# Two side-by-side recurrence lanes, one PSUM bank each, in layer 0 of a hybrid RWKV / gated-delta trunk

## The chip, the cores and the metric

The kernel runs on one core of a Trainium2 chip. The metric is the device time of one execution, in microseconds; a measurement is the median of several executions. The engines are called as in the profile: PE is TensorE (matmuls; PEld are its weight loads), DVE is VectorE, ACT is ScalarE, POOL is GpSimd and SP is SyncE, which issues most DMAs.

## The reference

A two-layer streaming encoder over 1024 frames of width 1024. Layer 0 is the one that matters here. One input projection feeds two groups of heads:

```
A = RWKV-7: 8 heads x 64        state = state*w + (state a) b' + v k' ; y = state r   (per frame)
B = gated DeltaNet: 4 heads x128  chunkwise WY form, state carried from chunk to chunk
out = concat(A, B) @ w_out, then MLP and a gated per-layer embedding
```

For group A the reference scans frame by frame (`wkv7_scan`). For group B it works on chunks: it solves a unit lower triangular system in each chunk, then runs

```
v_new = uc - wc @ state
o     = qd @ state + qkc @ v_new
state = state * gl + kd' @ v_new
```

over the chunks in order. The kernel treats both groups in the same way, in chunks of 128 frames: all that a chunk needs besides the incoming state is prepared ahead (scores, an inverse of a triangular matrix, decays), and a short chain of products carries the state through the chunks.

## The kernel before, in words

All matrix products of the projections are done with operands split in a high and a low part (tiles `whi`, `wlo`, `xg`), in 128x512 pieces into PSUM tiles called `dps` ("dense" work). PSUM has eight banks of 2 KB per partition, and here two are for dense work (tag `dense`), two for transposes and sums (tag `tp`), and one each for `ch`, `iz`, `pm` and `y`.

Layer 0 works on 16 units. A unit is a pair of RWKV heads or one gated-delta head (`p` is 0 to 3) in one half of the frames (`hf` is 0 or 1, 512 frames, four chunks); RWKV and gated-delta units alternate (`units`, L539). Each unit goes through five stages, written as Python generators that yield at places where the engine order may switch to something else:

- *in* (`l0_in`): the projections of the unit, the dense work. At the start of each half, x is loaded, scaled and split, and two low-rank projections ("lora", tiles `lwa` and `lg`) are made. Two weights, `wa2` and `g2` (128x512 each), are loaded once, in the first half.
- *front*: decays, normalised keys, score matrices, the first steps of the inverse.
- *mid* (`inverse_end`): the rest of the inverse, written into the tile `F`. There is one `F` for eight blocks (RWKV) and one for four (gated delta), in bank `iz`.
- *back* (`rwkv_back`, `gdn_back`): the chain over the four chunks.
- *post*: normalisation, gate, store to `yd`.

A lane (`l0_lane`) takes the units through one stage, in order. `Trunk.run` sets the order in which instructions are issued on all engines at once: it keeps a clock of its own, in which only matmuls advance time, and goes on with the first lane in its list whose due time has come; a yield says by name how long the lane should stay away, from a table of latencies (`"rwkv_back4": 0.64` and so on). Lanes earlier in the list have priority. Before, the list is post, back, mid, front (two lanes, for even and odd units), the sums for the gated-delta decays, and in. So there is one back lane: the RWKV and gated-delta chains follow one another. Mid may be two units ahead of back (`slack` 2).

The chain of one RWKV chunk (L949 to L990). The scaled state `Sh` is made by DVE (L953) from `S`; the products into `pw` (two with the scores `PMQ`, one with `Sh`) are copied by ACT to `W` (L963); the products of `X` (the inverse) with `W` give `pu`, which DVE scales into `U` (L971); the products of `tm` (transposed keys) with the values and `U` give `pu2`, from which DVE makes the new state (L987). Five more products per chunk give the outputs in `py`. `pw`, `pu` and `pu2` are tiles of bank `ch`, one after the other; `py` is a tile of bank `y` and holds the outputs of all four chunks, until ACT copies it once per unit to a tile `o` (L995) and squares it from PSUM into another (L997). The function `scores` (PMQ, L931) of the next chunk is called between.

The chain of one gated-delta chunk (L1142 to L1160). `pw` is one product of the keys with the state `Sg`; DVE makes `W` (L1147); `pu` is the inverse times `W`; ACT scales it to `U` (L1152); `p2` is the product of the keys with `U`, from which DVE makes the state in place (L1158); two products per chunk go to `po` in bank `y`, copied and squared once per unit (L1163, L1165). `pw`, `pu` and `p2` are tiles of bank `ch` here too, so that the two kinds of chain share both banks.

Every matmul is recorded on the helper's line L177, every transpose on L192; a matmul of two f32 operands appears as two records. The helper `together` ties matmuls in a given order without a semaphore.

Of the kernel before, what the change touches and what calls it, by code (L numbers as in the profile page):

```python
# [8 lines left out]
F32 = mybir.dt.float32  # L9
# [22 lines left out]
L0_BACK = {"gate": 2, "b": 14, "tm": 3, "o": 3}  # L32
# [77 lines left out]
class Trunk:  # L110
    def __init__(self, ctx, tc, a, dbg=None, stop=None):
        self.ctx, self.tc, self.nc, self.a = ctx, tc, tc.nc, a
        self.dbg, self.stop = dbg or {}, stop

        self.now, self.done, self.lat = 0.0, {}, LAT
        self.nd, self.rx, self.late, self.extra = -1, None, None, []

        self.steps, self.begun = [], None
# [385 lines left out]
    def layer0_in(self):  # L504
        nc, tc, a = self.nc, self.tc, self.a
        with ExitStack() as es:
# [60 lines left out]
    def l0_in(self, units):  # L567
# [3 lines left out]
        for u, (nm, p, hf) in enumerate(units):  # L571
            if u % 8 == 0:
# [25 lines left out]
                if hf == 0:  # L598
                    self.wa2 = fr.tile([P, 512], F32, tag="wa2", name="wa2")
                    nc.sync.dma_start(out=self.wa2, in_=a["wa2"])  # L600
                    self.g2 = self.l0.tile([P, 512], F32, tag="g2", name="g2")
                    nc.sync.dma_start(out=self.g2, in_=a["g2"])
# [6 lines left out]
                if hf == 0:  # L609
# [3 lines left out]
                    self.extra = [lambda t=t: self.psm.tile([P, HB], F32, tag=t, name="dps") for t in ("y", "ch", "pm")]  # L613
# [184 lines left out]
    def rwkv_front(self, p, hf, sc, raws, u):  # L798
# [20 lines left out]

        psw, psa = ptile(), ptile()  # L820
        self.together([self.mm(ps, self.wa2[r, p * P:(p + 1) * P], sc["lwa"][r], start=True, stop=True)
# [88 lines left out]
    def rwkv_mid(self, p, hf, sc, st, u):  # L910
        yield from self.inverse_end(st["X"], st["N"], 8, self.F[8])
        return dict(st, F=self.F[8])

    def rwkv_back(self, p, hf, sc, st, u):
# [33 lines left out]
        py = psm.tile([P, HB], F32, tag="y", name="py")  # L948

        for c in range(4):  # L950
# [7 lines left out]
            pw = psm.tile([P, HB], F32, tag="ch", name="ch")  # L958
            for h in range(2):
                self.mm(pw[:, hs[h]], pmq[c, h][:, 1, :], Vt[:, c, hs[h]], start=h == 0, stop=False)  # L960
            self.mm(pw[:, 0:P], AR[:, c, 0, :], Sf, start=False, stop=True)
            W = h2.tile([P, P], F32, tag="W", name="W", bufs=2)
            A.copy(W, pw[:, 0:P])  # L963
# [3 lines left out]
            pu = psm.tile([P, HB], F32, tag="ch", name="ch")  # L967
            U = h2.tile([P, P], F32, tag="U", name="U", bufs=2)
            for h in range(2):
                self.mm(pu[:, hs[h]], X[:, 4 * h + c, :], W[:, hs[h]], start=True, stop=True)  # L970
            V.tensor_tensor(U.rearrange("p (h i) -> p h i", h=2), pu[:, 0:P].rearrange("p (h i) -> p h i", h=2),  # L971
                            cc[:, 2 * c:2 * c + 2].rearrange("p (h o) -> p h o", o=1).broadcast_to((P, 2, 64)),
                            op=ALU.mult)
            py_c = py[:, c * C:(c + 1) * C]
            self.mm(py_c, Sf, AR[:, c, 1, :], start=True, stop=False)
            yield "rwkv_back5"

            pu2 = psm.tile([P, HB], F32, tag="ch", name="ch")
# [7 lines left out]
            S2 = h2.tile([P, 64], F32, tag="S2", name="S2", bufs=2)  # L986
            V.scalar_tensor_tensor(S2, S, ee[:, c:c + 1], pu2[:, 0:64], op0=ALU.mult, op1=ALU.add)  # L987
            S = S2
# [5 lines left out]
        yc = t2(tag="o")  # L994
        A.copy(yc, py)  # L995
        sy = t2(tag="o")
        A.activation(sy, py, AF.Square)  # L997
# [3 lines left out]
    def rwkv_post(self, p, hf, sc, st, u):  # L1001
        nc, sm, V = self.nc, self.sm, self.nc.vector
        t2 = self.t2
        yc, sy, bon = st["yc"], st["sy"], st["bon"]
        pv = self.post_bank()
# [18 lines left out]
        self.mm(pg, self.g2[:, p * P:(p + 1) * P], sc["lg"], start=True, stop=True)  # L1024
# [107 lines left out]
    def gdn_mid(self, n, hf, sc, st, u):  # L1132
        yield from self.inverse_end(st["X"], st["N"], 4, self.F[4])
        return dict(st, F=self.F[4])

    def gdn_back(self, n, hf, sc, st, u):
# [4 lines left out]
        po = psm.tile([P, HB], F32, tag="y", name="po")  # L1141
        for c in range(4):  # L1142
            i = c
            pw = psm.tile([P, HB], F32, tag="ch", name="ch")
            self.mm(pw[:, 0:P], KQ[:, c, 0, :], S, start=True, stop=True)
            W = h2.tile([P, P], F32, tag="W", name="W", bufs=2)
            V.scalar_tensor_tensor(W, pw[:, 0:P], sc["egc"][:, i, n:n + 1], vt[:, c, :], op0=ALU.mult, op1=ALU.add)  # L1147
            yield "gdn_back0"
            pu = psm.tile([P, HB], F32, tag="ch", name="ch")
            self.mm(pu[:, 0:P], X[:, c, :], W, start=True, stop=True)  # L1150
            U = h2.tile([P, P], F32, tag="U", name="U", bufs=2)
# [949 lines left out]
```

## Time and profile before

| | us |
|---|---|
| median of 3 runs | 3112.31 |
| lowest and highest | 3107.09, 3116.35 |
| the profiled execution | 3119.22 |
| its span in the profile | 3117.5 |
| mean granted TensorE clock | 0.968 |

The profile is of one execution. Its span runs from the first to the last instruction, and 1.7 us of the execution lie outside it. The page gives busy times by engine; a view of waits says which instruction an engine stood idle for, and which engine's work ended that wait; a view of windows gives busy times and clock by stage; a view of lines groups equal instructions; the timeline shows single instructions. An interval of idle time in square brackets at the end of a timeline row is the time for which that engine was idle ahead of it.

### The profile page before, as it was taken

What the parts mean: (1) busy time and instruction counts of PE and PEld (TensorE: products, weight loads), DVE (VectorE), ACT (ScalarE), POOL (GpSimd) and SP (SyncE); (2) the same over time, 40 slices, a digit from 0 to 9 for tenths busy, and PEclk for the clock granted to TensorE, in tenths of its full rate; (3) what the DMA queues carried; (4) which work ended last, traced back from release to release, by engine and by line L of the source; (5) the groups of instructions that cost most, each with busy time, mean ns of one, the idle gap of its engine ahead of it and who ended that gap; (6) DMA issues with size and microseconds to landing.
All of it is one profiled execution on the core that took longest, in us unless ns stands there. A gap on an engine that the chain in (4) does not pass through costs nothing.

```text
span 3117.5 us, 47104 instructions
## 1 busy us (share of the span) xinstructions
PE 2998.6 (96%) x17288; PEld 2477.6 (79%) x17288; DVE 2222.7 (71%) x4518; ACT 1512.2 (49%) x2922; POOL 534.0 (17%) x978
## 2 busy tenths in 40 slices
PE   7999999999999999999999999999899999999999
PEld 5777777777777788888887988888788788888887
DVE  6646675667758788877866676776768688888862
ACT  4323433344436544544433577777766545444431
POOL 6524442443510000000005111110210000000002
PEclk8989999999999999999999999999999999999999
DMA  4212112212356444754424111110256444754433
GB/s 137 71 42 72 44 58 72 63 51 70 103 168 206 148 156 150 259 168 153 126 98 136 52 33 33 42 46 16 71 176 215 147 152 149 246 179 147 135 108 102
DMA packets 187639, 358.45 MB, mean 115 GB/s; under 512 B 45712, under 2 KB 47888, under 8 KB 187408
## 3 DMA queue, kind: packets, MB, share of 16 engines
q1 hardware_dynamic: 158608, 303.00, 30.0%
q10 hardware_dynamic: 28800, 52.44, 4.4%
q8 instruction: 136, 2.23, 0.3%
q14 instruction: 95, 0.78, 0.1%
HBM read 262.04 MB, written 93.32 MB: 114 GB/s over the span
## 4 chain that ended last, share of the span: by engine, by line
PE 81%; DVE 9%; ACT 4%; DMA 3%; issue 1%; POOL 1%; SPq 0%; DVEq 0%; POOLq 0%; ACTq 0%
PE dps L177 68%; PE ch L177 2%; PE po L177 2%; PE iz L177 1%; PE pm L177 1%; PE tp L177 1%; PE pt L192 1%; DVE ptile L350 1%; PE py L177 1%; PE sn L177 1%; DVE pb L1941 1%; ACT pb L1954 1%; PE pp L177 1%; DMA wraw<-in_w_out 1%; PE st L177 1%
## 5 line engine op out<-in xcount | busy, mean ns | idle before, releaser
L177 PE MATMUL dps<-r,act 128*128 128x512 f32 x3528 | 831.5, 393 | 0.0
L177 PEld LDWEIGHTS dps<-r,act 128*128 128x128 f32 x3528 | 664.8, 189 | 146.7
L177 PE MATMUL dps<-xg,whi 128*128 128x512 f32 x1280 | 439.7, 424 | 12.7 <-ACT xg L352 7.4
L1598 POOL TENSOR_TENSOR pn<-pn,prs 128x512 f32<-128x512 f32 x32 | 45.0, 1409 | 1577.1 <-ACT prs L386 1480.0
L177 PE MATMUL dps<-wq,act 128*128 128x384 f32 x1536 | 306.4, 345 | 6.9 <-DVE vs L1850 3.1
L177 PEld LDWEIGHTS dps<-xg,whi 128*128 128x128 f32 x1280 | 237.2, 198 | 64.8 <-ACT xg L352 7.4
L177 PEld LDWEIGHTS dps<-wq,act 128*128 128x128 f32 x1536 | 266.7, 191 | 11.1 <-DVE vs L1850 5.3
L177 PE MATMUL dps<-xg,wlo 128*128 128x512 f32 x640 | 260.1, 407 | 1.3 <-DVE wlo L304 1.3
L177 PE MATMUL dps<-late,act 128*128 128x512 f32 x960 | 229.2, 392 | 0.0
L177 PEld LDWEIGHTS dps<-late,act 128*128 128x128 f32 x960 | 180.3, 188 | 39.7
L1271 ACT CAST act<-act 128x512 fp32r<-128x512 f32 (+1 forms) x223 | 137.6, 649 | 129.3 <-PE dps L177 60.7
L1374 DVE TENSOR_TENSOR late<-late,dps 128x512 f32<-128x512 f32 x224 | 152.3, 684 | 62.5 <-PE dps L177 54.2
L1271 ACT CAST act<-late 128x512 fp32r<-128x512 f32 x210 | 124.1, 618 | 136.3 <-PE dps L177 91.1
L177 PE MATMUL dps<-act 128*128 128x512 f32 x672 | 165.5, 393 | 0.1
L1272 DVE TENSOR_TENSOR act<-act 128x512 fp32r<-128x512 f32 (+1 forms) x223 | 154.5, 719 | 4.2 <-ACT act L1271 4.2
L177 PEld LDWEIGHTS dps<-xg,wlo 128*128 128x128 f32 x640 | 125.9, 197 | 32.1 <-issue 2.3
L177 PEld LDWEIGHTS dps<-act 128*128 128x128 f32 x672 | 126.1, 188 | 29.2 <-DVE xw L1506 0.5
L1272 DVE TENSOR_TENSOR act<-late,act 128x512 fp32r<-128x512 f32 x210 | 141.4, 687 | 10.9 <-ACT act L1271 9.0
L303 ACT CAST whi<-wraw 128x1024 fp32r<-128x1024 f32 x78 | 81.9, 1050 | 122.4 <-PE dps L177 83.2
L1506 DVE TENSOR_TENSOR xw<-xw,dps 128x512 f32<-128x512 f32 x174 | 117.7, 681 | 29.6 <-PE dps L177 29.6
L177 PE MATMUL dps<-xw,act 128*128 128x512 f32 x576 | 138.4, 391 | 0.0
L1379 ACT ACTIVATE late<-late 128x512 f32<-128x512 f32 x128 | 80.2, 629 | 117.1 <-DVE late L1374 106.8
(482 smaller groups left out, 5652.0 us busy)
## 6 DMA issues: line engine op xcount, KB each, us to landing
hb<-late ACTq DMA_DIRECT2D x168, 256.0 KB
act<-hb SPq DMA_DIRECT2D x138, 256.0 KB
late<-in_w SPq DMA_DIRECT2D x60, 512.0 KB
wraw<-in_w_in SPq DMA_DIRECT2D x56, 512.0 KB
act<-in_w SPq DMA_DIRECT2D x96, 256.0 KB
braw<-hb SPq DMA_DIRECT2D x72, 256.0 KB
wraw<-in_w_out SPq DMA_DIRECT2D x21, 512.0 KB
wraw<-in_w_qkv SPq DMA_DIRECT2D x21, 512.0 KB
```

Source lines behind the costliest of these rows:

```text
L177: return self.begin(self.nc.tensor.matmul(out, lhsT, rhs, start=start, stop=stop, skip_group_check=again))
L192: return self.begin(self.nc.tensor.transpose(out, in_, ident))
L303: nc.scalar.copy(hi, raw)
L350: nc.vector.tensor_tensor(dst[:, 1, sl], src, dst[:, 0, sl].bitcast(F32), op=ALU.subtract)
L1271: A.copy(hi, s)
L1272: V.tensor_tensor(lo, s, hi.bitcast(F32), op=ALU.subtract)
L1374: V.tensor_tensor(r, t, u, op=ALU.add)
L1379: A.activation(t, t, AF.Relu)
L1506: V.tensor_tensor(x[n][:, hs[hf]], x[n][:, hs[hf]], ps, op=ALU.add)
L1598: G.tensor_tensor(pn, pn, prs[:, sl], op=ALU.mult)
L1941: V.tensor_tensor_reduce(S, pn[:, 0:nn * P], toep[:, (3 - nn) * P:], op0=ALU.add, op1=ALU.max, scale=1.0, scalar=NEG, accum_out=mx[:, 0:1])
L1954: A.activation(S, S, AF.Exp, bias=mx[:, 2:3], accum_out=l[:, 0:1])
```

## The change

1. *Lanes.* The back lane becomes two: one for the even units (RWKV), one for the odd (gated delta). Mid may now be four units ahead of back. The planner's list of lanes whose steps it notes (`ahead`) grows by one.
2. *Banks.* RWKV's chain keeps bank `ch`, gated delta's gets `cg` in place of `y`. Each holds its four products of a chunk in four regions of 128 columns: `pw`, `pu`, `pu2` (or `p2`), and the output (`py`, `yo`). A new helper `behind` ties all matmuls into one of these banks in their order of issue.
3. *Outputs.* ACT copies the output of each chunk (128x128) from the bank to the tile `o`; the square reads that tile.
4. *Order in a chunk.* RWKV: the state `S2` is made ahead of the five output products. Gated delta: the state is made behind both output products.
5. *Tiles.* Two inverse tiles of each size, used in turn (`F[8, e]`, `F[4, e]`, the first of them in the tile of the pool `pre` with the tag `pl`). `W` and `U` have one buffer each, and gated delta its own (`Wg`, `Ug`); `tm` goes from three to two buffers, `o` from three to five.
6. *Loads.* `wa2` and `g2` are loaded for each RWKV unit as 128x128 pieces. Since `pl` is taken, the x tiles of the second half come through `ph` (two of four) and `wraw`, and those for the squares through `ph` alone.

```diff
-L0_BACK = {"gate": 2, "b": 14, "tm": 3, "o": 3}
+L0_BACK = {"gate": 2, "b": 14, "tm": 2, "o": 5}
...
+    def behind(self, key, ins):
+
+        if key in self.last:
+            self.together([self.last[key], ins])
+        self.last[key] = ins
...
-            self.F = {G: l0.tile([P, G, P], F32, tag=f"F{G}", name=f"F{G}") for G in (4, 8)}
+            self.F = {(G, e): l0.tile([P, G, P], F32, tag=f"F{G}{e}", name=f"F{G}") for G, e in ((4, 0), (4, 1), (8, 1))}
+            self.F[8, 0] = self.pre.tile([P, 8, P], F32, tag="pl", name="F8")
...
-            self.run([self.l0_lane(units, "post", "back", 0), self.l0_lane(units, "back", "mid", 0), self.l0_lane(units, "mid", "front", 2),
+            self.run([self.l0_lane(units, "post", "back", 0), self.l0_lane(units, "back", "mid", 0, 0, 2),
+                      self.l0_lane(units, "back", "mid", 0, 1, 2), self.l0_lane(units, "mid", "front", 4),
                       self.l0_lane(units, "front", "in", 0, 0, 2), self.l0_lane(units, "front", "in", 0, 1, 2),
-                      self.gdn_cums(), self.l0_in(units)], ahead=(1, 2))
+                      self.gdn_cums(), self.l0_in(units)], ahead=(1, 2, 3))
...
-                    x2 = [self.load_x(q, self.pre if q < 2 else self.wp, "ph" if q == 0 else "pl" if q == 1 else "wraw")
-                          for q in range(4)]
+                    x2 = [self.load_x(q, self.wp if q in (1, 2) else self.pre, "wraw" if q in (1, 2) else "ph") for q in range(4)]
...
-                    x2 = self.load_x(q, self.pre, "pl" if q % 2 else "ph")
+                    x2 = self.load_x(q, self.pre, "ph")
...
+        wa2 = fr.tile([P, P], F32, tag="wa2", name="wa2")
+        nc.sync.dma_start(out=wa2, in_=self.a["wa2"][:, p * P:(p + 1) * P])
...
@@ rwkv_back, one chunk @@
-        py = psm.tile([P, HB], F32, tag="y", name="py")
+        bank = psm.tile([P, HB], F32, tag="ch", name="ch")
+        pw, pu, pu2, py = bank[:, 0:P], bank[:, P:2 * P], bank[:, 2 * P:2 * P + 64], bank[:, 384:512]
+        yc = t2(tag="o")
...
-            self.mm(py_c, Sf, AR[:, c, 1, :], start=True, stop=False)
             yield "rwkv_back5"
...
                 for h in range(2):
-                    self.mm(pu2[hs[h], 0:64], t[:, c, hs[h]], v[:, hs[h]], start=t is Ktm, stop=t is Btm)
+                    mm(pu2[hs[h]], t[:, c, hs[h]], v[:, hs[h]], start=t is Ktm, stop=t is Btm)
+            S2 = h2.tile([P, 64], F32, tag="S2", name="S2", bufs=2)
+            V.scalar_tensor_tensor(S2, S, ee[:, c:c + 1], pu2, op0=ALU.mult, op1=ALU.add)
+            S = S2
+            mm(py, Sf, AR[:, c, 1, :], start=True, stop=False)
             for v, j in ((Vt[:, c], 2), (U, 0)):
                 for h in range(2):
-                    self.mm(py_c[hs[h]], v[:, hs[h]], pmq[c, h][:, j, :], start=False, stop=j == 0)
+                    mm(py[hs[h]], v[:, hs[h]], pmq[c, h][:, j, :], start=False, stop=j == 0)
+            A.copy(yc[:, c * C:(c + 1) * C], py)
...
-        A.copy(yc, py)
         sy = t2(tag="o")
-        A.activation(sy, py, AF.Square)
+        A.activation(sy, yc, AF.Square)
...
+        g2 = self.l0.tile([P, P], F32, tag="g2", name="g2")
+        nc.sync.dma_start(out=g2, in_=self.a["g2"][:, p * P:(p + 1) * P])
...
@@ gdn_back, one chunk @@
-            yo = po[:, c * C:(c + 1) * C]
-            self.mm(yo, S, qd[:, c, :], start=True, stop=False)
-            p2 = psm.tile([P, HB], F32, tag="ch", name="ch")
-            self.mm(p2[:, 0:P], kd[:, c, :], U, start=True, stop=True)
-            V.scalar_tensor_tensor(S, S, sc["egl"][:, i, n:n + 1], p2[:, 0:P], op0=ALU.mult, op1=ALU.add)
-            self.mm(yo, U, QK[:, c, :], start=False, stop=True)
+            mm(p2, kd[:, c, :], U, start=True, stop=True)
+            mm(yo, S, qd[:, c, :], start=True, stop=False)
+            mm(yo, U, QK[:, c, :], start=False, stop=True)
+            V.scalar_tensor_tensor(S, S, sc["egl"][:, i, n:n + 1], p2, op0=ALU.mult, op1=ALU.add)
+            A.copy(o[:, c * C:(c + 1) * C], yo)
```

More of the change, by code (lines that the diff above doesn't have):

```diff
@@ L598, in l0_in @@
                 if hf == 0:
[L599 to L602, printed above, removed]
                     self.hv = self.l0.tile([P, 2, 4], F32, tag="hv", name="hv")
@@ L611, in l0_in @@
                     self.rs = fr.tile([P, HB], F32, tag="rsbc", name="rsbc", bufs=2)
-                    self.extra = [lambda t=t: self.psm.tile([P, HB], F32, tag=t, name="dps") for t in ("y", "ch", "pm")]
+                    self.extra = [lambda t=t: self.psm.tile([P, HB], F32, tag=t, name="dps") for t in ("cg", "ch", "pm")]
                     self.late, self.plan = [], {2: lambda: self.row_stats([acc], rsc), 3: lambda: self.to_rows(rsc, self.rs)}
@@ L910, in rwkv_mid @@
     def rwkv_mid(self, p, hf, sc, st, u):
-        yield from self.inverse_end(st["X"], st["N"], 8, self.F[8])
-        return dict(st, F=self.F[8])
+        F = self.F[8, u // 2 % 2]
+        yield from self.inverse_end(st["X"], st["N"], 8, F)
+        return dict(st, F=F)
     def rwkv_back(self, p, hf, sc, st, u):
@@ L957, in rwkv_back @@
             Sf = Sh.rearrange("p h i -> p (h i)")
-            pw = psm.tile([P, HB], F32, tag="ch", name="ch")
             for h in range(2):
[L960 to L963, printed above, removed]
+                mm(pw[:, hs[h]], pmq[c, h][:, 1, :], Vt[:, c, hs[h]], start=h == 0, stop=False)
+            mm(pw, AR[:, c, 0, :], Sf, start=False, stop=True)
+            W = h2.tile([P, P], F32, tag="W", name="W")
+            A.copy(W, pw)
             if c < 3:
@@ L1132, in gdn_mid @@
     def gdn_mid(self, n, hf, sc, st, u):
-        yield from self.inverse_end(st["X"], st["N"], 4, self.F[4])
-        return dict(st, F=self.F[4])
+        F = self.F[4, u // 2 % 2]
+        yield from self.inverse_end(st["X"], st["N"], 4, F)
+        return dict(st, F=F)
     def gdn_back(self, n, hf, sc, st, u):
@@ L1140, in gdn_back, with mm @@
         KQ, vt, kd, qd, QK, cs, X = (st[x] for x in ("KQ", "vt", "kd", "qd", "QK", "cs", "F"))
-        po = psm.tile([P, HB], F32, tag="y", name="po")
+        bank = psm.tile([P, HB], F32, tag="cg", name="cg")
+        pw, pu, p2, yo = (bank[:, q * P:(q + 1) * P] for q in range(4))
+        o = self.t2(tag="o")
+        def mm(*args, **kw):
+            self.behind("cg", self.mm(*args, **kw))
         for c in range(4):
             i = c
[L1144 to L1147, printed above, removed]
+            mm(pw, KQ[:, c, 0, :], S, start=True, stop=True)
+            W = h2.tile([P, P], F32, tag="Wg", name="W")
+            V.scalar_tensor_tensor(W, pw, sc["egc"][:, i, n:n + 1], vt[:, c, :], op0=ALU.mult, op1=ALU.add)
```

32 lines of the change are left out of this document (12 added, 20 removed).

## The prediction

> **What bounds the kernel now.** I read the page first, then the waits of TensorE in the first 930 us, then the stages by windows, then the groups by line, and last two short stretches of the timeline. The changed lines belong to layer 0, which fills the span up to about 930 us; everything behind it is untouched.
>
> ```profile
> span 3117.5 us, 47104 instructions
> PE 2998.6 (96%) x17288; PEld 2477.6 (79%) x17288; DVE 2222.7 (71%) x4518; ACT 1512.2 (49%) x2922; POOL 534.0 (17%) x978
> ```
>
> The reader is to see that TensorE (PE) is busy 96% of the whole span: a change of order can win only its idle time, its slow-clock time and the overhead inside its busy time. VectorE (DVE) has room left, ScalarE (ACT) has half its time free.
>
> The windows split the first millisecond. The columns are the length, then for each engine the busy time and the count, then the granted clock, the DMA share and GB/s.
>
> ```profile
> 0.00:30.00 30.00, 20.46 (x75) 15.67 (x76) 15.15 (x18) 16.22 (x25) 25.75 (x86) 0.94 0.56 195
> 30.00:100.00 70.00, 61.05 (x282) 48.19 (x282) 46.91 (x97) 28.76 (x51) 44.07 (x59) 0.90 0.31 92
> 100.00:200.00 100.00, 93.57 (x743) 71.29 (x742) 44.89 (x94) 29.36 (x64) 37.99 (x95) 0.81 0.20 59
> ...
> 300.00:400.00 100.00, 94.62 (x819) 72.57 (x819) 68.10 (x164) 41.90 (x88) 45.64 (x98) 0.92 0.18 54
> ...
> 600.00:700.00 100.00, 98.75 (x924) 74.80 (x924) 61.19 (x148) 40.26 (x89) 43.54 (x114) 0.95 0.18 56
> ...
> 900.00:950.00 50.00, 46.56 (x231) 36.28 (x232) 26.45 (x50) 21.11 (x36) 0.00 (x0) 1.00 0.55 174
> ...
> sum 1000.00, PE 947.69 PEld 735.36 DVE 646.47 ACT 402.77 POOL 384.12; mean PE 78.97 PEld 61.28 DVE 53.87 ACT 33.56 POOL 32.01
> ```
>
> TensorE is idle for 1000 - 947.7 = 52.3 us of the first millisecond, 18.5 us of that before 100 us (30 - 20.46 and 70 - 61.05), where no recurrence runs yet. Some 34 us are left for all of the pipeline's gaps. What ends them is in the waits (time in all, times, longest):
>
> ```profile
> PE dps L192 <- DVE f L714: 8.7, 1, 8.7
> ...
> PE ch L177 <- DVE U L971: 5.6, 7, 2.5
> PE pm L177 <- DVE PMQ L931: 4.1, 5, 1.5
> ...
> PE ch L177 <- DVE Sg L1158: 2.3, 6, 0.9
> ...
> PE ch L177 <- ACT W L963: 1.9, 1, 1.9
> ...
> PE ch L177 <- ACT U L1152: 1.5, 3, 1.1
> ...
> PE pm L177 <- ACT tm L943: 0.7, 1, 0.7
> ...
> PE ch L177 <- DVE S L987: 0.2, 1, 0.2
> ```
>
> All rows but the first belong to the recurrences: 5.6 + 4.1 + 2.3 + 1.9 + 1.5 + 0.7 + 0.2 = 16.3 us in 7 + 5 + 6 + 1 + 3 + 1 + 1 = 24 waits, 0.68 us each. So the chains' latency, which a second lane could cover, costs 16.3 us before, about 0.5% of the span; most of the rest is already hidden behind the projections' matmuls (dps).
>
> **The change part by part.** The price of one link in a chain (last product, reader, next product) has two ends in the trace:
>
> ```profile
> 379.41 0.49 PE L177 MATMUL ch<-Sh,AR 128*128 128x128 f32 x2
> ...
> 379.99 0.27 ACT L963 COPY W<-ch 128x128 f32<-128x128 f32 x1 [1.49 <-PE ch L177]
> ...
> 580.60 0.49 PE L177 MATMUL ch<-Sh,AR 128*128 128x128 f32 x2
> ...
> 582.71 0.62 ACT L893 CAST bh<-f 128x512 fp32r<-128x512 f32 x1 [3.99 <-DVE f L890]
> 583.24 0.26 ACT L963 COPY W<-ch 128x128 f32<-128x128 f32 x1
> ...
> 583.55 0.66 PE L177 MATMUL ch<-W,F 128*128 128x64 f32 x4 [1.86 <-ACT W L963]
> ```
>
> With the reader's engine free, the products end at 379.41 + 0.49 = 379.90 and the copy at 380.26: 0.36 us. With another ScalarE job ahead of it, the products end at 581.09 and the next begin at 583.55: 2.46 us. A link costs what of this no TensorE work between the two products covers.
>
> *Added waits.* Each chain now lives in one bank, and all accesses to it follow each other. In the order of the changed kernel the first product of a next chunk waits for ScalarE's copy of the outputs (27 RWKV and 27 gated-delta places, 24 of each inside a unit), and the five RWKV output products wait for the new state S2 (32 places); before, the outputs had a bank of their own, were read once per unit, and a next chunk waited for the state alone. Between these pairs I counted the TensorE work that the order puts there. Behind the RWKV copy 12 of the 24 inner places have under 0.5 us of cover; behind S2, 6 of 32; gated delta's copy has at least 0.85 us everywhere, so I cost it at nothing (if that cover goes, at most 24 x 0.68 = 16.3 us). Priced at the 0.68 us that a wait of this kind took: copies 12 x 0.68 = 8.2 us, S2 6 x 0.68 = 4.1 us. Ends: nothing, if dense work is always ahead; (12 + 6) x 2.46 = 44 us, if ScalarE is always taken. I stay near the low row, since ACT idles 60% of this stage (402.77 of 1000).
>
> *Old links, reordered.* The same count of places with short cover, before and after: gated delta's U 3 and 7, its W 0 and 1, RWKV's U 5 and 3, its W 3 and 1, PMQ 7 and 14; the state Sg has 9 short places before and none after. So U and W of gated delta add 5 x 0.68 = 3.4 us, RWKV's take off 4 x 0.68 = 2.7 us, the Sg row (2.3 us) goes, and PMQ, whose 7 short places cost 4.1 us, doubles by 4.1 us. Together +2.5 us; the ends are -16.3 us, all links covered, and 17 new short places (4 + 1 + 7, and 5 in the inverse's TZ, which I cost at nothing because none of its 2 short places before waited) times 2.46 = 42 us, which cannot all come true.
>
> *Operations.* The rows are count, busy time and mean ns:
>
> ```profile
> L1070 ACT ACTIVATE f<-KQ 128x512 f32<-128x512 f32 x16 | 9.9, 621 | 0.6 <-DVE KQ L1061 0.5
> ...
> L963 ACT COPY W<-ch 128x128 f32<-128x128 f32 x32 | 8.6, 270 | 48.7 <-PE ch L177 48.5
> ...
> L997 ACT ACTIVATE o<-py 128x512 f32<-128x512 f32 x8 | 4.8, 604 | 0.0
> ...
> L1163 ACT COPY o<-po 128x512 f32<-128x512 f32 x8 | 4.7, 589 | 9.4 <-PE po L177 9.3
> L995 ACT COPY o<-py 128x512 f32<-128x512 f32 x8 | 4.7, 587 | 1.8 <-PE py L177 1.6
> ```
>
> Sixteen output copies of 0.59 us become 64 of 128x128, by the W row 0.27 us: 17.3 us for 9.4 us, +7.9 us of ScalarE. The 16 squares read the copied tile in place of the bank, +0.02 us each by the KQ row. ScalarE does this in its idle 60%, so beyond the waits above it costs nothing; without that cover it is 8 us. The products, the state updates and the dense matmuls keep their number. The second inverse tiles add four sets of zeroing at the start on POOL, where it lies ahead of the squares of x.
>
> *Start.* The chain of waits into the 8.7 us wait is
>
> ```profile
> 49.35 1.90 POOL wraw L697
> 51.26 0.02 issue
> 51.28 1.05 ACT whi L303
> ...
> 59.28 0.60 DVE f L714
> 59.88 0.04 issue
> 59.92 0.59 PE dps L192 x4
> ```
>
> POOL's scaling of the third lora weight begins at 49.35 us behind squares of x. In the new order only one square stands ahead of it, not five, and f L714 comes three places earlier on VectorE. I take 3 us off; the ends are 0 and the whole wait, 8.7 us. What is late next is the same chain from the first lora weights on.
>
> *Loads.* wa2 and g2 come as 16 loads of 128x128 in place of two of 128x512, issued a unit ahead of use, or (g2) before the output's store; x for the second half comes through other tiles, one of them free only after q0 is split. At a DMA share of 0.18 to 0.20 in the stages where they fall they are hidden: 0. What waits behind them on SyncE's queue is the weight and scratch loads; one late x tile would cost about what the first split costs at the start:
>
> ```profile
> PE dps L177 <- ACT xg L352: 7.4, 1, 7.4
> ```
>
> that is 0 to 7.4 us.
>
> *Clock.* In 100 to 200 us the granted clock is 0.81 with 6.4 us idle, in 600 to 700 us 0.95 with 1.3 us idle; in 900 to 950 us it is 1.00 with 3.4 us idle, so idle time in many short pieces tells, but not in proportion. I put no sum on it. Its upper end: from the 0.95 of most stages down to 0.92 (the row of 300 to 400 us) over 800 us, 24 us. The Trainium skill ("TensorE: Matmul & The Clock Gate", part 1, "The HAM clock gate") says that throttling is the resting state and recent activity lifts it; the trace agrees only in part, the 1.00 of 900 to 950 us being the row against it, and by this rule the new waits would cost more than their length.
>
> *Sum:* 8.2 + 4.1 + 2.5 - 3 = +11.8 us. Against the profiled execution (3119.22 us, of which 1.7 us lie outside the span) that is 3131.0; this execution is 6.9 us above the median of 3112.31, on which the forecast stands: 3112.3 + 11.8 = **3124 us**.
>
> One rule of the Trainium skill bears on the first term: "PSUM — Partial Sum Buffer", section "PSUM bank collisions raise a hardware error", has PSUM guarded by bank and partition quadrant, not by address. It speaks against four regions in one bank: by it the waits of the copies and of S2 are there to stay, however disjoint the columns, while regions guarded by address would need neither and leave 2.5 - 3 = -0.5 us, no change. In 378 to 383 us no product touches a bank while its reader does, which agrees but does not test it.
>
> **The rivals.**
> 1. *Faster.* The two lanes' chunks fall between each other, each link is covered by the other chain, and TensorE never waits on a chain: the 16.3 us of waits and 3 us of the start go, 3112.3 - 19.3 = 3093 us, and up to half of the 24 us of the clock term more if the stages rise instead of falling, 3081. It decides at the cover of a link: with more than 0.7 us of the other chain's work at every link it wins. For it: separate banks and W, U tiles, so nothing but order ties the chains. Against: the order still runs a gated-delta chunk beside an RWKV chunk in a few places only. 0.22.
> 2. *No change.* The change does not do what it says: the inverse ahead of each chain still sets its start, the chains alternate as before, and the copies hide behind dense matmuls. Then only the start and a link here and there move: 3112 within 9 us. 0.22.
> 3. *Much slower.* The copies stand behind 1.05 us casts on ScalarE, and each short place costs the long price: 18 x 2.46 = 44 us, - 3 us, 3153 us. For it: the row of 583.24 us. Against: 24 waits of before averaged 0.68 us. 0.14.
>
> **How the numbers follow.** The forecast case (added waits at their usual price, 3124 us, of itself 3108 to 3138) has 0.42. About 0.3% of the time, 9.3 us, is what a measurement of this kernel can tell from no change. Of the forecast case three quarters lie above that (0.32) and one quarter within (0.10). Slower: 0.32 + 0.14 = 0.46. Same: 0.10 + 0.22 + 0.02 of the first rival = 0.34. Faster: 0.20. The range goes from 3088 us, into the first rival, to 3150 us, forecast plus clock end.
>
> **What would show it.** Right: rows of the outputs' copy (`ch` waiting on ACT) with some 8 us in a dozen waits, a row of `ch` or its output products waiting on DVE S2 with some 4 us, the Sg row gone, PMQ near 8 us, the 8.7 us wait of the start near 6 us, PE idle in the first millisecond up by about 12 us, 3130 us profiled. Wrong: chain waits below 10 us in all, or a clock in 100 to 900 us that moves by more than 0.02 either way, or a stage behind 950 us that moves at all.

## The result, and the profile after

The changed kernel takes 3138.63 us (median of 4 runs, 3130.53 to 3144.26), the kernel before in the same series 3109.7 us (4 runs). The ratio is 1.0076, with a 95% interval of 1.0052 to 1.0100: slower by 16 to 31 us (28.9 us between the two medians). The forecast was 3124 us, 12 us over before, in a range of 3088 to 3150: the sign and the range hold, the size was about half of what came. A range 62 us wide would have held no change as well.

The page of the changed kernel:

```profile
span 3142.3 us, 47255 instructions
PE 3000.2 (95%) x17288; PEld 2478.2 (79%) x17288; DVE 2233.4 (71%) x4518; ACT 1518.1 (48%) x2970; POOL 524.1 (17%) x984
```

TensorE does the same 17288 instructions in the same busy time (3000.2 us against 2998.6). The span is 24.8 us longer, so the difference is idle time. To see where it is, I took from each trace the moment by which the first 2000 matmul records into `dps` have begun, which is near the end of layer 0's changed part: 951.2 us before, 973.6 us after, 22.4 us later. Behind it the changed kernel loses only 2.4 us of the 24.8 (2168.7 us against 2166.3). These are the sums of a view of windows up to that moment, before and after; the first number is the time, the second TensorE's busy time.

```profile
sum 951.20, PE 898.89 PEld 695.43 DVE 600.13 ACT 367.62 POOL 384.12; mean PE 449.45 PEld 347.72 DVE 300.07 ACT 183.81 POOL 192.06
```

```profile
sum 973.60, PE 901.85 PEld 695.18 DVE 608.75 ACT 374.56 POOL 376.78; mean PE 450.92 PEld 347.59 DVE 304.37 ACT 187.28 POOL 188.39
```

TensorE's idle time rises from 951.20 - 898.89 = 52.3 us to 973.60 - 901.85 = 71.8 us: 19.5 of the 22.4 us. Two stages of the changed kernel show that a part of it comes before any recurrence:

```profile
30.00:100.00 70.00, 55.38 (x258) 44.18 (x257) 39.88 (x86) 24.97 (x45) 36.32 (x55) 0.88 0.28 85
100.00:200.00 100.00, 96.47 (x746) 74.30 (x744) 51.93 (x108) 33.88 (x73) 40.24 (x98) 0.81 0.22 64
```

In 30 to 100 us TensorE is busy for 55.4 us, where it was busy for 61.1. Half of that comes back at once: in 100 to 200 us it is busy for 96.5 us, where it was busy for 93.6, and the first chunk's products into `ch` come at 136 us instead of 98. The waits of TensorE in the changed kernel (us in all, times, longest) are

```profile
PE pm L177 <- DVE PMQ L937: 10.3, 5, 3.5
PE ch L177 <- DVE U L980: 9.7, 6, 4.0
PE dps L198 <- DVE f L717: 8.8, 1, 8.8
PE dps L177 <- ACT xg L358: 7.5, 1, 7.5
PE ch L177 <- ACT o L995: 4.9, 7, 2.3
PE ch L177 <- DVE S L989: 4.4, 6, 1.6
...
PE cg L177 <- ACT U L1163: 1.9, 6, 0.5
...
PE cg L177 <- DVE W L1159: 1.0, 1, 1.0
...
PE cg L177 <- ACT o L1169: 0.7, 2, 0.4
...
PE ch L177 <- ACT W L973: 0.4, 1, 0.4
```

The rows of the two chains (`ch`, `cg`, `pm`) sum to 10.3 + 9.7 + 4.9 + 4.4 + 1.9 + 1.0 + 0.7 + 0.4 = 33.3 us in 34 waits, where 24 waits took 16.3 us. The output copies (`o`) and the new state (`S`) have rows, as forecast; the wait for the state Sg is gone; but the rows of U and PMQ, to which the forecast gave +1.4 us (-2.7 for RWKV's U and W, +4.1 for PMQ), grew by 10.3 us together. The start's wait (8.7 us) is still there (8.8 us).

### The profile page after: what moved, and what is told of

Read it like the earlier page. It is cut to its first block, busy times and chain, and to the rows that moved or that the text cites. A ratio compares the mean times of both kernels' runs of the same rounds, so it can differ in the third digit from the quotient of the medians.

```text
span 3142.3 us, 47255 instructions
## 1 busy us (share of the span) xinstructions
PE 3000.2 (95%) x17288; PEld 2478.2 (79%) x17288; DVE 2233.4 (71%) x4518; ACT 1518.1 (48%) x2970; POOL 524.1 (17%) x984
## 4 chain that ended last, share of the span: by engine, by line
PE 77%; DVE 11%; ACT 4%; DMA 4%; issue 2%; POOL 1%; SPq 0%; DVEq 0%; ACTq 0%; POOLq 0%
PE dps L177 65%; PE ch L177 2%; PE pm L177 1%; PE iz L177 1%; PE tp L177 1%; PE cg L177 1%; PE po L177 1%; DVE ptile L356 1%; PE pt L198 1%; PE sn L177 1%; ACT pb L1962 1%; DMA wraw<-in_w_qkv 1%; DVE pb L1949 1%; PE pp L177 1%; DMA late<-in_w 1%
```

## The experiments

All ratios are to the kernel before, run on the same chip in the same series, with 95% intervals. 0.1% is 3.1 us.

| kernel | ratio | interval | TensorE idle to the 2000th dense record, us | over before at equal clock, us (estimate) |
|---|---|---|---|---|
| before | 1 | | 52.3 | 0 |
| changed | 1.0076 | 1.0052 to 1.0100 | 71.8 | not on record |
| e3: one back lane | 1.0059 | 1.0042 to 1.0076 | 73.6 | 19 |
| e4: mid two ahead | 1.0066 | 1.0053 to 1.0078 | 71.5 | 20 |
| f5: single inverse tiles, one lane | 1.0049 | 1.0031 to 1.0066 | 67.9 | 16 |
| e1: loads alone | 1.0032 | 1.0014 to 1.0050 | 56.4 | 4 |
| e2: x tiles as before | 1.0073 | 1.0058 to 1.0089 | 68.6 | 15 |
| f1: banks alone | 1.0066 | 1.0044 to 1.0087 | 68.9 | 15 |
| f3: copies don't read the bank | 1.0049 | 1.0027 to 1.0070 | 59.0 | 9 |
| k1: outputs in the other bank | 1.0008 | 0.9990 to 1.0026 | 54.1 | 0 |
| k2: the same, tied | 1.0085 | 1.0058 to 1.0111 | 62.4 | 14 |
| k6: whole change, outputs in the other bank | 1.0041 | 1.0022 to 1.0059 | 53.3 | 8 |
| g1: chains side by side, latency 28 | 1.0220 | 1.0196 to 1.0244 | 90.6 | 29 |
| g2: latency 28 alone | 1.0217 | 1.0189 to 1.0246 | 99.2 | 39 |

The idle column is worked out as above, from the sums of windows of each profiled execution.

The last column is an estimate from the times and the mean granted clocks of all executions of a series. In each of the four series one straight line, with a step for each kernel, fits them to 2.5 to 2.8 us; the time falls by 2.4 to 2.5 us for each 0.001 of granted clock. The column is a kernel's step above the kernel before, to within 2 to 5 us. What a ratio has beyond it went with a lower clock. Whether a kernel brought that about or met it by chance is not shown, except for g1 and g2: all their executions (0.954 to 0.963) lie below all of before in their series (0.966 to 0.976).

The instruction order is made anew for each kernel, on all engines. Only e3, e4 and f5 have the order of the changed kernel; each of the others has one of its own. So most experiments, e1 too, compare whole orders, and not a single wait.

My theory after the result had two parts: the waits inside the shared bank, and a start that became later. Its rivals were the lanes themselves, and the loads.

### The lanes, the slack and the second inverse tiles do nothing (e3, e4, f5)

```diff
# e3
-self.l0_lane(units, "back", "mid", 0, 0, 2), self.l0_lane(units, "back", "mid", 0, 1, 2),
+self.l0_lane(units, "back", "mid", 0),
...
# e4
-self.l0_lane(units, "mid", "front", 4)
+self.l0_lane(units, "mid", "front", 2)
# f5: as e3 and e4 together, and
-... F8 and F4 twice
+self.F[4, 1], self.F[8, 1] = self.F[4, 0], self.F[8, 0]
```

> The changed kernel with one back lane in place of two (mid still four ahead); banks, regions, copies, tiles and loads as changed. Theory A (the loss is the waits inside one bank and the start): +20 to +29 us over before, with ch waits on the output copies and on S2 of 9 us or more. Theory C (two lanes make the planner put the links of a chain closer together): most of it goes, +6 us or less beyond the start.

> The changed kernel with mid two units ahead of back in place of four. Theory A: no part in the loss, +24 to +30 us over before. Rival (mids far ahead compete with the chains for TensorE and use up the cover): +10 to +18 us, with fewer PMQ and U waits.

> The change without its tile and lane part: one inverse tile of each size, one back lane, mid two ahead; banks, copies and loads as changed. Its instruction order on every engine is that of the changed kernel, so +18 to +26 us over before, as the changed kernel; it serves beside the kernel with the outputs in the other bank as the changed kernel on the same chip.

e3 gave 3127.35 us, e4 3130.29 us and f5 3126.43 us against 3109.8 to 3114.3 us of before. In all three the order of the instructions is that of the changed kernel on every engine (f5 only moves POOL's zeroing of the tiles at the start). The times came out at or under the low end of what was expected of them; it is the order that decides. So the second lane never comes into play: units come to the back stage one at a time. The planner counts 46.33 us (`end_front` in its table) from the end of a unit's front to its inverse, and the inverse is what a chain waits for; a shorter count alone does not bring two units together either (g2, below). In the trace of the changed kernel the chains stand in a row: RWKV's chain ends at 297 us, the second unit of gated delta has its products from the inverse on in `cg` from 311 to 337 us, and RWKV's next chain goes on with its inverse at 352 us. Only a unit's first products, which need no inverse, come ahead (299 us for RWKV, 353 us for gated delta's third unit). With one lane or two, a chain finds the one before it all but finished.

These kernels also serve as three more measurements of the changed kernel: with its own, +0.49 to +0.76% in three series, some 15 to 24 us, and 16 to 20 us at equal clock. Their idle time agrees within 6 us; their time to the same dense record (959.4 to 973.6 us) varies more, with the granted clock (0.94 or 0.95 in that stage). Two of them:

```profile
sum 964.50, PE 890.94 PEld 686.17 DVE 608.08 ACT 374.68 POOL 377.46; mean PE 445.47 PEld 343.09 DVE 304.04 ACT 187.34 POOL 188.73
```

```profile
sum 964.10, PE 892.62 PEld 687.64 DVE 607.84 ACT 375.15 POOL 378.23; mean PE 446.31 PEld 343.82 DVE 303.92 ACT 187.57 POOL 189.12
```

The first is e3, the second e4. Of one and the same order, TensorE is busy for 901.9, 890.9 and 892.6 us, and idle for 71.8, 73.6 and 71.5 us: to compare two orders, idle time is the steadier reading.

### The loads alone (e1, e2)

e1 is the kernel before with wa2 and g2 loaded per unit and the x tiles as in the change; e2 is the changed kernel with the x tiles as before (and therefore one `F[8]`).

```diff
# e2
-x2 = self.load_x(q, self.pre, "ph")
+x2 = self.load_x(q, self.pre, "pl" if q % 2 else "ph")
...
```

> The kernel before with the load part of the change alone: wa2 and g2 loaded per RWKV unit, the x tiles of the squares through one tile (ph), the x tiles of the second half through wraw and ph. Theory A (the profile of after shows 6 us more dense work outstanding at 75 us, behind ScalarE squares that wait for an x load): +6 us, about 3116 against 3110. Theory B (loads are hidden, the whole loss is in the chains): within 2 us of before.

> The changed kernel with its x tiles as before (squares through ph and pl, second half as before), which leaves room for one inverse tile F[8] only; two lanes, banks and the rest as changed. Theory A: 6 us better than the changed kernel, about +21 us over before, with the wait for f at the start near 9 us and no PMQ wait of 3.5 us in the first 100 us. Theory B: as the changed kernel, +27 us. If the second F[8] tile mattered, more than +27.

e1 costs 0.14 to 0.50%, some 10 us, but only 4 us at equal clock: its executions had 0.966 to 0.974, those of before 0.969 to 0.976. e2 lost the PMQ wait of 3.5 us (its longest is 1.8 us), and 1.0073 is theory A's +21 us within its interval; but the changed kernel's own order (e4) had 1.0066 in the same series, so by time undoing the x loads took nothing off. Nor do the parts add up by time: loads 0.32%, banks 0.66% (f1, below), together 0.49 to 0.76%. At equal clock both come right: e2 lies 4 to 5 us below e3 and e4 (15 against 19 and 20), and loads and banks (4 and 15) give what the three kernels of the changed order have (16 to 20).

At the start of the changed kernel one way in which a load reaches TensorE can be read, in its chain of waits ahead of 62 us (start, length, what):

```profile
51.32 2.18 POOL acc L668
53.50 0.02 issue
53.51 4.19 DMA xr<-in_x
...
58.32 0.61 ACT xr L666
58.94 0.10 ACT em L842
...
61.27 0.59 DVE f L717
```

The x tiles of the second half's squares now pass through one tile. The next load starts only when POOL has added up the square before (53.5 us), takes 4.2 us, and ScalarE's square of it stands in ScalarE's queue ahead of `em`, which the decays and in the end `f` wait for. That this is what the loads cost is not shown. In e1, which has the same loads, no load stands in the chain ahead of `f`, and the wait for `f` is 6.5 us, less than the 8.7 of before; its new waits in the first 100 us are one of 3.1 us for PMQ and one of 2.5 us into `tp`. And in f1, which has the loads of before, an x load (3.8 us) stands in that chain. In e1 TensorE's idle time rises by 4.1 us in an execution of 3119.66 us, which agrees with the 4 us at equal clock.

### The banks alone (f1)

f1 is the kernel before with the chains' text of the change (banks, regions, copies, order in a chunk, `o` in four buffers), and lanes, tiles, slack and loads as before.

```diff
# made from the changed kernel; beside this the lanes, tiles, slack and loads of before
-L0_BACK = {"gate": 2, "b": 14, "tm": 2, "o": 5}
+L0_BACK = {"gate": 2, "b": 14, "tm": 2, "o": 4}
```

> The bank part of the change alone: one bank per chain in four regions, outputs copied per chunk, state ahead of the output products, o in four buffers; one back lane, one inverse tile of each size, mid two ahead, all loads as before. Theory A (waits inside the bank): +10 to +15 us over before, with ch waits on the output copy and on S2 of 8 us or more. Theory B (the loads carry it all): within 5 us of before.

3136.27 against 3114.83 us, 1.0066: the bank part alone costs as much as the whole change, more than theory A's 10 to 15 us. The `behind` ties have no part in it: the program without them has the same order on all engines (it was not run). The waits of f1:

```profile
PE ch L177 <- DVE U L982: 9.7, 6, 4.0
...
PE pm L177 <- DVE PMQ L939: 7.0, 8, 1.6
...
PE ch L177 <- ACT o L997: 3.1, 8, 0.8
...
PE ch L177 <- DVE S L991: 2.7, 6, 0.8
```

The copy and the state take 5.8 us here, less than the 8 us of theory A; U is again at 9.7 us. So the waits that the profile puts down to the bank are not the larger part of the 16.6 us of idle time that f1 has over before.

### The copies' waits alone (f3)

```diff
-A.copy(yc[:, c * C:(c + 1) * C], py)
+A.copy(yc[:, c * C:(c + 1) * C], py if c == 3 else W)
# and the same with yo in gdn_back
```

> The changed kernel, but the output copies of the first three chunks of each unit read W in place of the bank: ScalarE does the same copies, and nothing in the bank waits for them. This leaves out three quarters of the recurrences' output. Theory A: the rows of 4.9 and 0.7 us go, some 5 us better than the changed kernel, +13 to +17 us over before. Rival (the wait is replaced by that for S2 just ahead of it, or the order shifts): no better than the changed kernel, +20 us.

3127.75 us, 1.0049 (0.27 to 0.70%). The copy's row goes, and S's falls to 0.4 us with it; U is at 9.0 us in 9 waits, PMQ at 3.4 us. Against the four measurements of the changed kernel (1.0049 to 1.0076) the time does not tell 5 us from nothing; the idle time (59.0 against 67.9 to 73.6 us) says that some 10 us of waiting went, and the estimate at equal clock (9 us against 16 to 20) agrees. Since f3 has an order of its own, with more than a tenth of TensorE's products elsewhere, this is not the price of the copies' rows alone.

### The outputs in the other bank (k1, k2, k6)

Since the chains hardly meet, the other chain's bank is all but free while one runs. k1 puts the output products there and leaves their place open; k2 keeps them tied where the change has them. Both are made from f1.

```diff
# k1 and k2, RWKV (gated delta likewise, yo in "ch")
-pw, pu, pu2, py = bank[:, 0:P], bank[:, P:2 * P], bank[:, 2 * P:2 * P + 64], bank[:, 384:512]
+pw, pu, pu2 = bank[:, 0:P], bank[:, P:2 * P], bank[:, 2 * P:2 * P + 64]
+py = psm.tile([P, HB], F32, tag="cg", name="py")[:, 0:P]
# k1 only
-mm(py, Sf, AR[:, c, 1, :], start=True, stop=False)
+self.mm(py, Sf, AR[:, c, 1, :], start=True, stop=False)
# and the other output products of both chains in the same way
```

> The bank part alone, but each chain's output products go to the other chain's bank (py to cg, yo to ch), which stands idle meanwhile since the chains follow one another; they are not tied to the chain's order. State-first order, copies per chunk and all tiles as in the bank part. Theory A (outputs in the chain's own bank cost the time): the ch and cg waits on the output copy and on S2 go, U falls towards 6 us, time within 6 us of before. Rival F (copies on ScalarE or the new order in the chunk cost it): +15 us or more, as the bank part.

> As the kernel with the outputs in the other bank, but the output products stay tied in their place behind S2's products and ahead of the next chunk. Theory A1 (what costs is the waiting on semaphores within the bank): within 6 us of before, like the untied one. Theory A2 (what costs is that the output products can no longer stand in the gaps of the chain, where they covered links): U stays near 9 us or more and the time at +10 to +20 us.

k1 takes 3112.79 us against 3110.68 us of before, 1.0008 (-0.10 to +0.26%): the whole loss of the bank part is gone, with the 64 copies, the single W and U and the state-first text still there. k2 takes 3143.2 us, 1.0085, more than the 10 to 20 us of theory A2. The texts of the two differ in nothing but the tie, and a kernel that frees only the products which do not need U (the state's and the values') has the same order as k1 on every engine.

What these products do is seen in one chunk, at the same place of the work. k1 first, then k2 (start, length, groups of TensorE and two of VectorE; in brackets the idle time ahead):

```profile
270.19 0.38 PE L177 MATMUL ch<-Sh,AR 128*128 128x128 f32 x2
270.41 0.39 PE L177 MATMUL py<-AR,Sh 128*128 128x128 f32 x2
270.72 0.44 PE L177 MATMUL py<-PMQ,b 128*64 128x128 f32 x4
...
272.31 0.66 PE L177 MATMUL ch<-W,F 128*128 128x64 f32 x4
...
274.06 0.28 DVE L983 TENSOR_TENSOR U<-ch,cc 128x128 f32<-128x128 f32 x1
274.26 0.73 DVE L814 SCALAR_TENSOR_TENSOR f<-raw,vecs,f 128x512 f32<-128x512 f32 x1
...
274.39 0.34 PE L177 MATMUL ch<-b,tm 128*64 128x64 f32 x4 [1.05 <-DVE U L983]
```

```profile
270.92 0.38 PE L177 MATMUL ch<-Sh,AR 128*128 128x128 f32 x2
...
272.45 0.66 PE L177 MATMUL ch<-W,F 128*128 128x64 f32 x4
...
274.11 1.57 DVE L814 SCALAR_TENSOR_TENSOR f<-raw,vecs,f 128x512 f32<-128x512 f32 x1
...
275.67 0.28 DVE L983 TENSOR_TENSOR U<-ch,cc 128x128 f32<-128x128 f32 x1
...
276.00 0.48 PE L177 MATMUL ch<-b,tm 128*64 128x64 f32 x4 [2.52 <-DVE U L983]
...
276.63 0.80 PE L177 MATMUL py<-AR,Sh 128*128 128x128 f32 x2
277.35 0.70 PE L177 MATMUL py<-PMQ,b 128*64 128x128 f32 x4
```

In k1 the outputs of state and values stand behind `ch<-Sh,AR` and are done while ScalarE copies W: 0.7 us of work in a gap that is there anyway. In k2 TensorE has them still to do behind U. But that U is waited for 2.52 us in place of 1.05 does not come from their absence: the products with W begin at 272.31 and 272.45 us, and it is VectorE that begins U 1.6 us later, behind L814, which in k1 stands behind U. The tie has moved VectorE's order as well. Over the recurrences U's row is 2.9 us in k1 and 9.2 us in k2:

```profile
PE ch L177 <- DVE U L983: 2.9, 5, 1.1
```

```profile
PE ch L177 <- DVE U L983: 9.2, 8, 2.7
```

That the outputs' place decides, with the order that follows from it, and not their bank, is shown by the times of f1, k1 and k2. That they cost by covering links no longer, as theory A2 has it, is not shown. At equal clock every kernel in which they are tied, by the chain's bank or by hand, costs 14 to 20 us (f1, k2, e2 and the three of the changed order; f3, tied as well but with no wait for most copies, 9), and those in which they are free 0 to 8 (k1, e1, k6). The chains' rows of waits sum to 12.9 us in k2 and to 20.4 us in k1 (PMQ 8.3 us against 1.0, a W of 3.3 us): links that grew in one place shrank in another, because the tie moves more than a tenth of TensorE's products to another place in the order. What rose in k2 are the waits into the inverse (`iz`, 12.9 us against 6.8) and into the transposes (`tp`, 9.2 against 3.3). The idle time up to the 2000th dense record is 8 us more in k2 (62.4 against 54.1), and the rest of the 25 us between the two executions lies in busy time (915.3 against 898.6 us, at granted clocks of 0.92 and 0.93); that execution of k2 took 3150.76 us, the longest of its runs. The clock is part of k2's loss by time: its six executions had 0.964 to 0.971, k1's twelve 0.967 to 0.979, and at 0.970 and 0.971 k2 took 3130.2 and 3127.1 us, k1 3115.4 to 3118.4.

k6 is the whole change with the outputs so placed.

```diff
# on the changed kernel, as k1 on f1
+py = psm.tile([P, HB], F32, tag="cg", name="py")[:, 0:P]
+self.mm(py, Sf, AR[:, c, 1, :], start=True, stop=False)
```

> The whole change (lanes, loads, tiles, copies), but each chain's output products go to the other chain's bank and are not tied to the chain's order. Theory G (the bank of the outputs is the cause, the loads cost what they cost alone): +4 to +12 us over before. Theory H (bank and loads do not add up; the loads cost nothing with this order): within 4 us. Rival F (something else in the change): +18 us or more.

3124.84 us against 3109.84 us, 1.0041 (0.22 to 0.59%), where f5, the changed kernel's order, had 1.0049 in the same series. Its idle time is that of before (53.3 us; an execution of 3112.98 us, 12 us less than its median). What it still costs by time, 7 to 18 us, reaches over the 4 to 12 us of theory G and is not told apart from the changed kernel. At equal clock it costs 8 us against f5's 16 in the same series: half of the loss is gone. Of the 8, the loads alone account for some 4 (e1); the rest stays open.

### Chains made to run side by side (g1, g2)

```diff
# g1 and g2
-    "end_front": 46.33,
+    "end_front": 28.0,
# g1 only, in l0_lane
+            if stage == "back" and u % 2 == 0:
+                yield ("mid", u + 1)
```

> The changed kernel with two lines more: RWKV's back stage waits until the mid stage of the next unit is done, so that both chains start together, and the planner's latency behind front is 28 in place of 46.33, so that this holds nothing up. Chunks of the two chains then alternate chunk by chunk (some 157 changes between them in TensorE's order in place of 32). Theory O (overlap covers the links): chain waits (ch, cg, pm) below 15 us against 33 in the changed kernel, and a time 10 to 20 us below it, within 10 us of before. Rival P (dense work already covers what can be covered; overlap only bunches the chains and leaves other stretches bare): the chain waits fall little, or the time is no better than the changed kernel, +20 us or more over before.

> Control for the kernel with overlap: the changed kernel with the planner's latency behind front at 28 in place of 46.33, nothing else. The chains still follow one another (28 changes). Theory O: as the changed kernel, +15 to +25 us over before. Rival: the inverse comes too early, TensorE waits for its tiles (iz on T or on Xp), +30 us or more.

3184.86 and 3186.11 us: by time no difference between chains that alternate chunk by chunk and chains in a row; at equal clock the overlap takes some 9 us off (29 against 39). The overlap does what it should: the wait for U behind `ch` falls from 7.2 us in g2 to 0.5 us in g1. Its largest waits of the inverse and the chains are

```profile
PE iz L177 <- ACT T L448: 18.4, 6, 4.8
PE pm L177 <- DVE PMQ L939: 11.4, 6, 5.8
...
PE ch L177 <- DVE S L991: 2.5, 4, 1.0
...
PE cg L177 <- ACT o L1171: 2.1, 2, 1.4
```

All rows of `ch`, `cg` and `pm` sum to 18.9 us in g1 and to 29.2 us in g2. Much of what is won there is given back in the inverse (18.4 against 14.8 us in its largest row), in PMQ (11.4 against 6.4 us) and in waits for weight casts (whi, 6.6 against 2.3 us). Both take some 50 us more than the changed kernel. That the inverse is called before its data are back is a part of it: that `iz` row was 3.3 us in the changed kernel, and the idle time is 19 and 27 us more. The busy time is up too (919 us each against 902, in a stage granted 0.90 and 0.91 against 0.94); why the clock is lower is not shown. So the control missed its +15 to +25 us (its rival held). Theory O missed its time, and its 15 us for the chains' rows by 3.9, though they fell well below the control's; rival P held for the time. No kernel here beats the one before.

## Why the prediction was right, and where its working failed

- **What bounds the kernel.** Right: TensorE's busy time did not move, idle time did (+19.5 us up to the 2000th dense record).
- **Added waits** (12.3 us forecast). The places were right, the sum a little high: copies 4.9 + 0.7 us in 9 waits where 12 had been counted, S2 4.4 us in 6 waits as counted; 10.0 us, 0.67 us each, as priced.
- **Old links, reordered** (+2.5 us forecast). This is the term that was mis-sized. Without the new rows the chain waits went from 16.1 to 10.3 + 9.7 + 1.9 + 1.0 + 0.4 = 23.3 us, +7.2 us. I priced every short place at 0.68 us; U now takes 9.7 / 6 = 1.6 us a time and PMQ 2.1 us, because the reader can stand behind other work of its engine. In the 4.02 us wait for U in the changed kernel it is one instruction:

```profile
273.53 0.66 PE L177 MATMUL ch<-W,F 128*128 128x64 f32 x4
...
273.94 3.55 DVE L868 SCALAR_TENSOR_TENSOR AR<-f,E 128x512 f32<-128x512 f32 x1
...
277.88 0.27 DVE L980 TENSOR_TENSOR U<-ch,cc 128x128 f32<-128x128 f32 x1
...
278.21 0.34 PE L177 MATMUL ch<-b,tm 128*64 128x64 f32 x4 [4.02 <-DVE U L980]
```

  This instruction is not long in itself: the eight of its line take 0.72 us at the median. POOL is busy from 273.72 to 276.99 us, and the instruction ends 0.5 us behind that; whether POOL held it is not shown.
- **What no term had** is the place of the output products. I counted what they would wait for (S2), and not what becomes of the order when they can no longer stand anywhere. Given another bank and a free place (k1), the bank part costs nothing; given the bank alone (k2), it costs 14 us at equal clock, hardly less than f1. The inverse's rows (`iz`), which the forecast put at nothing, went from 5.6 to 10.4 us in the changed kernel. Whether the outputs' lost cover or the rest of the moved order is the cause stays open.
- **Start** (-3 us forecast). Wrong in sign: the wait for `f` stayed at 8.8 us and TensorE did 6.2 us less in the first 100 us, 3.3 us less by 200 us. I followed POOL's queue, and not ScalarE's, on which the squares of the one-tile loads stand. Not all of it is the loads' doing: f1, with the loads of before, did 2.5 us less in the first 100 us.
- **Loads** (0 forecast, up to 7.4 us). The 0 was too low: 10 us alone by time (e1; 4 to 16), some 4 at equal clock, which is inside the end. The share of the DMA engines says nothing of a wait for a tile, such as the chain at the start of the changed kernel shows.
- **Operations.** Right: the 64 copies took 8.6 + 8.4 us by their rows, 0.27 and 0.26 us each, and k1 carries them all at no cost that could be measured.
- **Clock.** Right to put no sum on it: 0.968 in both profiled executions. But the reading of a stage's clock from its idle time does not hold: in 100 to 200 us the changed kernel was granted 0.81 with 3.5 us idle, and e3, with the same order, 0.97 with 3.7. That new waits would cost more than their length, which I had drawn from part 1 of the Trainium skill's "TensorE: Matmul & The Clock Gate", is hardly borne out by the changed kernel: 19.5 us more idle time went with 22.4 us more time. k2 and g1 are nearer to it: 10.1 us more idle time went with 26.5 us more time to the same record, and 38 with 58.
- **The bank rule.** By "PSUM — Partial Sum Buffer" of the Trainium skill, section "PSUM bank collisions raise a hardware error", PSUM is to be guarded by bank and quadrant, so the regions could not be independent. The program keeps to it (every access to the bank waits for the one before it), and k1, with the outputs in another bank, has no row of a copy among its waits, and none of an output product that waits for S2. That a region guarded by address would do was not tried.
- **The rivals.** The first falls with e3: there is no second lane in the order. The second had its premise right (the chains follow one another as before) and its time wrong, since the bank and order changed with it. The third did not come: RWKV's copies took 0.70 us a time (4.9 / 7), not 2.46.
- **Its signs.** Of the signs of being right, the rows came and the Sg row went; the start's wait (8.8 us, not 6), the idle time (+19.5 us, not 12) and the profiled execution (3144.26 us, not 3130) did not. Of the signs of being wrong, the chain waits did not fall and the clock in 100 to 900 us stayed at 0.93; the 2.4 us behind the 2000th record are, by the letter, a stage that moved. The sign rests on a term that came (10.0 us of 12.3). That the time stayed inside the range is in part luck: the place of the outputs, the inverse and the loads had nothing in the sum and all added, the 3 us of gain at the start did not come, and only a wide range could hold it.

## What to carry to other kernels

A product that nothing waits for is best left free in the order: tying it, by hand or by a bank that the chain uses, cost 14 to 15 us here at equal clock (k2, f1). Such a tie moves the order of every engine, so look at the readers' queues too before naming a cause. A second lane in a planner does nothing as long as the due times bring one unit at a time: look whether it changes the instruction order before costing it. When tiles are shared to make room, follow the engine that uses the late tile, and what stands behind it in that queue. Where the granted clock of every execution is on record, compare kernels at equal clock: here that made the parts add up which did not add up by time.

## What was not expected of the hardware

Four kernels with the same order of instructions came out between 3126.4 and 3138.6 us in three series, and their profiled executions spent 891 to 902 us busy on the same matmuls, at granted clocks of 0.94 and 0.95 in that stage, while idle time varied by 6 us. Over all executions of a series the time fell by 2.4 to 2.5 us for each 0.001 of granted clock. Differences under about 0.4% between two kernels need the trace and the clock here, not the time alone.
